# Modulation stretches at the highest priority, the half loaded last first, and four PSUM banks for the products instead of five

## The chip, the cores and the metric

The kernel runs on one core of a Trainium2 chip. The metric is the time of one execution on the device in microseconds (us). Five engines work side by side, each in its own fixed order: TensorE (PE in the profile; PEld is its weight load), VectorE (DVE), ScalarE (ACT), GpSimd (POOL), and SyncE (SP), which here only issues DMAs. They meet through semaphores.

## The reference

One layer of a decoder is computed for two groups that share all weights: a prompt of 256 tokens and a sample group of 8 sequences with one new token each, together 264 columns. The model width is 2048, all data are float32. In short:

```
mod = silu(c) @ w_ada + b_ada                  # c: 1 + 8 rows; six parts of 2048: sh1 sc1 gt1 sh2 sc2 gt2
h = rmsnorm(x) * (1 + sc1) + sh1
q, k, v, u, ga, gb = split(h @ w_in)           # 9216 columns
o = dilated window attention, 12 heads in three groups (prompt: over itself; sample: over a cache)
p = multi-scale causal pooling of u, a linear map per group, a scale
x = x + gt1 * ((sigmoid(ga) * (o @ w_up_attn) + sigmoid(gb) * (p @ w_up_pool)) @ w_out)
h2 = rmsnorm(x) * (1 + sc2) + sh2
x = x + gt2 * (square(relu(h2 @ w_mlp_up)) @ w_mlp_down)
y = rmsnorm(x)                                 # and the updated caches of keys, values and pool inputs
```

## The kernel before, in words

**The products.** Each large matrix product holds the weights as the stationary operand, in tiles of 128 x 128, and streams the 264 columns. Weights and activations are each split into a high part of reduced precision and the rest: ACT casts the loaded weights to `whi` (L228), DVE subtracts to get `wlo` (L229), in pieces of 128 x 1024. A product is then three matmuls, L239 (high x high), L240 (high x rest) and L241 (rest x high), into one PSUM bank of the pool `mm`. In the text "a product" is one of these matmuls; there are 10,752 of them. Loads of 1 MB go through a pool of five buffers named `raw`, all issued by SP in the order of the program; a load is issued when the buffer it takes is free, either because DVE has split the weights that lay there or because PE has read them.

**The modulation.** `mod` is a product with 9 rows only, so there the loaded weights are the moving operand and `cT`, the 32-column block with silu(c), is the stationary one. Four such matmuls with 32 columns each run side by side in the array (`tile_position`), one for each quarter of the output, into the bank `pa`: L294 in `ada_pair`, which makes the first two parts in chunks of 1, 1, 2, 2, 2, 4 and 4 blocks of 128, just ahead of the chunk of `w_in` rows that needs them, and L345 in `ada_part`, which makes the other four parts in the background of the later stages, two loads at a time. `burst` gathers the matmuls of two loads and issues those of the second load first, the others behind them: a stretch of 32, 16 or 8 matmuls. The profile counts two records for one of them, so a stretch of 8 is x16 there. When a part is complete, ACT copies the sums to `adasb` (L251), PE turns them by transposes (L258, L315) into a bank of `mm`, and DVE adds the bias into `mods` (L263, L266).

**The stages.** The head (up to 22 us) loads x, transposes it (L436), computes the row norms and the first modulation chunk. Then come the first 5120 columns of `w_in` in seven chunks of rows, each accumulated into `qkv` by DVE, ACT or POOL as a bank fills (L516 to L526; a bank is filled by 3 products in the first two chunks, by 6 or 12 in the later ones); then the gates with pooling and the attention of the prompt woven between (L594 to L674), the attention of the sample (from L796 on), whose cache is loaded by DMAs that POOL issues (L700), then the products with `w_up_pool`, `w_up_attn` and `w_out`, and the MLP. After `w_out`, DVE and ACT update x, square it and add the squares into `sqa` (L914); PE sums the rows (L425, L426) for the second norm, and the first MLP products need `h2hi` and `h2lo`, which hold besides the activations ten columns with a part of `mods`.

**What sets the order.** The code is written in program order, and a scheduler of the framework puts each engine's instructions into the order that is executed. It follows a model of the engines and DMAs: of the instructions that are ready in the model, the one with the highest priority goes next, and without further notice that is the one written first. `tc.issue_after(i)` lets what is issued in the block come behind `i` on its engine. `tc.high_priority()`, which the change uses, puts what is issued in the block ahead of everything else that is ready. PSUM has eight banks: `psm` gives MB of them to products (name `mm`), `psa` one to the modulation (`pa`), and `psx` the remaining 7 - MB to all else, transposes and attention above all (`px`). The lines of the diff are L49, L268 to L274 and L288.

Of the kernel before, what the change touches and what calls it, by code (L numbers as in the profile page):

```python
# [45 lines left out]
UPR = 1  # L46
WO = (2, 3)
TW = (1, 3)
MB = 5  # L49
PI, PM = 4, 3  # L50
WARM = 6

# [70 lines left out]
def step_kernel(ctx, tc, x_prompt, x_sample, vectors, c_sample, kv0, kv1, kv2, state_pool, w_ada, w_in, w_up_attn,  # L123
# [12 lines left out]
    wsp = ctx.enter_context(tc.tile_pool(name="wsp", bufs=3))  # L136
    psm = ctx.enter_context(tc.tile_pool(name="psm", bufs=MB, space=bass.MemoryType.PSUM))
    psa = ctx.enter_context(tc.tile_pool(name="psa", bufs=1, space=bass.MemoryType.PSUM))
    psx = ctx.enter_context(tc.tile_pool(name="psx", bufs=7 - MB, space=bass.MemoryType.PSUM))

    def mm_tile(n=N):
        return psm.tile([128, 512], F32, name="mm")[:, :n]
# [102 lines left out]
    def flush():  # L245
        while pending:
            pending.pop()()

    def ada_block(src, cols):
        sb = adap.tile([128, 512], F32, name="adasb")  # L250
        nc.scalar.copy(sb[:, :cols], src[:, :cols])  # L251
        return sb

    def turn(sb, n):

        p = mm_tile(n * 128).rearrange("p (j c) -> p j c", j=n)
        for j in range(n):
            nc.tensor.transpose(p[:, j], sb[:, j * 128:(j + 1) * 128], ident)  # L258
        return p

    def set_mods(part, d0, m, p):
        n = m.shape[1]
        nc.vector.tensor_add(m, p, bT[:, part * 16 + d0:part * 16 + d0 + n, None].to_broadcast([128, n, 9]))  # L263
        if part in (1, 4):
            gv = (g_mix if part == 1 else g_mlp)[:, d0:d0 + n, None].to_broadcast([128, n, 9])
            nc.vector.tensor_mul(m, m, gv)  # L266

    def burst(raws, emit):  # L268

        last = emit(*raws[-1])  # L270
        for r in raws[:-1]:
            with tc.issue_after(last.ins):
                last = emit(*r)
        raws.clear()  # L274

    def ada_pair(d0, n, per=2):

        w = n * 128
        k = 1024 // w
        pa = psa.tile([128, 512], F32, name="pa")  # L280
        cols = 128 if n == 1 else w // 2
        each = KT // 2 if n == 1 else KT
        done = [0] * 4
        raws = []

        def emit(s, raw):
            for j in range(0, k, 2 if n == 1 else 1):
                for g in range(4):  # L288
                    if n == 1:
                        kt, src = s + j + g % 2, raw[:, g // 2, j + g % 2]  # L290
                    else:
                        kt, src = s + j, raw[:, g // 2, j, g % 2 * cols:(g % 2 + 1) * cols]
                    done[g] += 1
                    i = nc.tensor.matmul(pa[32 * g:32 * g + 32, :cols], cT[:, kt], src, start=done[g] == 1,  # L294
                                         stop=done[g] == each, tile_position=(0, 32 * g))
            return i

        for s in range(0, KT, k):
            raw = rawp.tile([128, 2048], F32, name="raw").rearrange("p (a k c) -> p a k c", a=2, k=k)
            for a in range(2):  # L300
                c0 = a * D + d0 * 128
                nc.sync.dma_start(raw[:, a], w_ada[s * 128:(s + k) * 128, c0:c0 + w].rearrange("(k p) c -> p k c", p=128))
            flush()
            raws.append((s, raw))
            if len(raws) == per:
                burst(raws, emit)
            if s + k < KT:
                yield
        sb = ada_block(pa, cols)

        def finish():
            nb = cols // 128
            if n == 1:
                p = mm_tile()[:, :18].rearrange("p (a b) -> p a b", b=18)
                nc.tensor.matmul(p[:, 0], sb[:, :128], sel2, start=True, stop=True)  # L315
                for part in range(2):
                    set_mods(part, d0, mods[:, part * 16 + d0:part * 16 + d0 + 1], p[:, :, part * 9:part * 9 + 9])
                return
            p = turn(sb, nb)
            for g in range(4):  # L320
                part, half = divmod(g, 2)
                dd = d0 + half * nb
                set_mods(part, dd, mods[:, part * 16 + dd:part * 16 + dd + nb], p[:, :, 32 * g:32 * g + 9])

        pending.append(finish)
        yield
# [9 lines left out]
    def ada_part(part):  # L336
# [12 lines left out]
        for kt in range(KT):  # L349
            v = load(w_ada[kt * 128:(kt + 1) * 128, part * D:(part + 1) * D], 1, D)  # L350
            flush()
            raws.append((kt, v))
            if len(raws) == 2:
                burst(raws, emit)
            if kt + 1 < KT:
                yield
# [320 lines left out]
    for kv in range(-1, 2):  # L677
        p = px([96, 128])
        nc.tensor.transpose(p, small[:, 1 + kv].rearrange("p h b -> p (h b)"), ident)
        r = ap.tile([96, 128], F32, name="rows", bufs=3)  # L680
# [364 lines left out]
    last = adap.tile([128, 512], F32, name="adasb")  # L1045
# [54 lines left out]
```

## Time and profile before

| | us |
|---|---|
| median of 3 runs | 1510.38 |
| lowest, highest | 1508.73, 1510.42 |
| the profiled execution | 1508.2 |
| its span, first to last instruction | 1506.4 |
| PE busy | 1484.2 |
| DVE busy | 875.4 |
| ACT busy | 668.3 |

Busy time counts from the start to the end of an instruction; matmuls overlap, so the time that a matmul costs is read from the start of one to the start of the next, not from its duration. Of an engine that waits, the profile tells how long it was idle and which instruction or DMA ended that. [...]

### The profile page before, as it was taken

What the parts mean: (1) busy time and instruction counts of PE and PEld (TensorE: products, weight loads), DVE (VectorE), ACT (ScalarE), POOL (GpSimd) and SP (SyncE); (2) the same over time, 40 slices, a digit from 0 to 9 for tenths busy, and PEclk for the clock granted to TensorE, in tenths of its full rate; (3) what the DMA queues carried; (4) which work ended last, traced back from release to release, by engine and by line L of the source; (5) the groups of instructions that cost most, each with busy time, mean ns of one, the idle gap of its engine ahead of it and who ended that gap; (6) DMA issues with size and microseconds to landing.
All of it is one profiled execution on the core that took longest, in us unless ns stands there. A gap on an engine that the chain in (4) does not pass through costs nothing.

```text
span 1506.4 us, 29357 instructions
## 1 busy us (share of the span) xinstructions
PE 1484.2 (99%) x12454; PEld 1398.6 (93%) x12454; DVE 875.4 (58%) x1404; ACT 668.3 (44%) x992; POOL 114.6 (8%) x175
## 2 busy tenths in 40 slices
PE   7999999999999999999999999999999999999997
PEld 6899999877899889899999999999999999999997
DVE  6876666544465437765855445545555555555765
ACT  5544433344444544454644444344343444434355
POOL 0334100010101001300000000000010000100000
PEclk9999999999999999999999999999999999999998
DMA  9979998888897778877666666677576685766541
GB/s 302 323 267 315 330 310 286 313 289 265 281 312 263 255 259 301 289 265 263 217 226 224 224 224 224 227 237 249 169 265 224 210 293 174 274 228 245 205 141 58
DMA packets 162931, 377.62 MB, mean 251 GB/s; under 512 B 7233, under 2 KB 33361, under 8 KB 153192
## 3 DMA queue, kind: packets, MB, share of 16 engines
q1 hardware_dynamic: 153152, 340.02, 65.8%
q0 software_dynamic: 4064, 33.03, 6.0%
q10 hardware_dynamic: 5584, 2.69, 0.6%
q8 instruction: 98, 1.61, 0.4%
q14 instruction: 33, 0.27, 0.0%
HBM read 370.74 MB, written 26.15 MB: 263 GB/s over the span
## 4 chain that ended last, share of the span: by engine, by line
PE 97%; ACT 1%; DMA 1%; DVE 0%; issue 0%; SPq 0%; ACTq 0%
PE mm L239 29%; PE mm L240 29%; PE mm L241 29%; PE pa L345 4%; PE pa L294 2%; PE px L654 1%; PE px L672 1%; DMA raw<-in_w_ada_dram 1%; PE px L636 0%; ACT whi L228 0%; PE px L1012 0%; PE px L667 0%; PE px L436 0%; PE px L833 0%; PE mm L258 0%
## 5 line engine op out<-in xcount | busy, mean ns | idle before, releaser
L229 DVE TENSOR_TENSOR wlo<-raw,whi 128x1024 fp32r<-128x1024 f32 x448 | 555.4, 1241 | 468.3 <-ACT whi L228 463.4
L228 ACT CAST whi<-raw 128x1024 fp32r<-128x1024 f32 x448 | 469.5, 1049 | 630.1 <-PE mm L240 541.0
L239 PE MATMUL mm<-hhi,whi 128*128 128x264 f32 x1152 | 331.8, 289 | 3.1 <-ACT whi L228 2.2
L240 PE MATMUL mm<-hlo,whi 128*128 128x264 f32 x1152 | 328.8, 286 | 0.0
L241 PE MATMUL mm<-hhi,wlo 128*128 128x264 f32 x1152 | 326.3, 285 | 0.0
L239 PE MATMUL mm<-h2hi,whi 128*128 128x264 f32 (+1 forms) x1024 | 292.1, 285 | 0.0
L241 PE MATMUL mm<-ffhi,wlo 128*128 128x264 f32 x1024 | 291.9, 285 | 0.0
L240 PE MATMUL mm<-h2lo,whi 128*128 128x264 f32 (+1 forms) x1024 | 291.7, 285 | 0.0
L240 PE MATMUL mm<-fflo,whi 128*128 128x264 f32 x1024 | 291.6, 285 | 0.0
L239 PE MATMUL mm<-ffhi,whi 128*128 128x264 f32 x1024 | 291.4, 285 | 0.0
L241 PE MATMUL mm<-h2hi,wlo 128*128 128x264 f32 (+1 forms) x1024 | 291.3, 285 | 0.0
L239 PEld LDWEIGHTS mm<-hhi,whi 128*128 128x128 f32 x1152 | 217.2, 189 | 19.9 <-issue 12.7
L240 PEld LDWEIGHTS mm<-hlo,whi 128*128 128x128 f32 x1152 | 217.5, 189 | 1.2 <-DVE gate_a L526 0.8
L241 PEld LDWEIGHTS mm<-hhi,wlo 128*128 128x128 f32 x1152 | 216.4, 188 | 0.3 <-issue 0.2
L239 PEld LDWEIGHTS mm<-h2hi,whi 128*128 128x128 f32 x1024 | 193.2, 189 | 4.2 <-ACT whi L228 2.5
L239 PEld LDWEIGHTS mm<-ffhi,whi 128*128 128x128 f32 x1024 | 193.5, 189 | 1.7 <-ACT xa L998 0.8
L240 PEld LDWEIGHTS mm<-fflo,whi 128*128 128x128 f32 x1024 | 193.5, 189 | 0.0
L241 PEld LDWEIGHTS mm<-h2hi,wlo 128*128 128x128 f32 x1024 | 192.6, 188 | 0.8 <-DVE wlo L229 0.8
L240 PEld LDWEIGHTS mm<-h2lo,whi 128*128 128x128 f32 x1024 | 192.8, 188 | 0.0
L241 PEld LDWEIGHTS mm<-ffhi,wlo 128*128 128x128 f32 x1024 | 192.4, 188 | 0.0
L239 PE MATMUL mm<-mhi,whi 128*128 128x264 f32 x256 | 73.5, 287 | 0.0
L240 PE MATMUL mm<-mlo,whi 128*128 128x264 f32 x256 | 72.8, 284 | 0.0
(279 smaller groups left out, 1379.9 us busy)
## 6 DMA issues: line engine op xcount, KB each, us to landing
raw<-in_w_in_dram SPq DMA_DIRECT2D x71, 1024.0 KB, 7.1
raw<-in_w_ada_dram SPq DMA_DIRECT2D x64, 1024.0 KB, 5.3
raw<-in_w_mlp_up_dram SPq DMA_DIRECT2D x64, 1024.0 KB, 5.5
raw<-in_w_mlp_down_dram SPq DMA_DIRECT2D x64, 1024.0 KB, 5.1
raw<-in_w_ada_dram SPq DMA_DIRECT2D x64, 512.0 KB, 6.9
raw<-in_w_out_dram SPq DMA_DIRECT2D x16, 1024.0 KB, 7.4
cv<-in_cache_kv_w_dram POOLq DMA_DIRECT2D x5, 1024.0 KB, 10.0
raw<-in_w_up_pool_dram SPq DMA_DIRECT2D x4, 1024.0 KB, 7.2
```

The lines of the kernel that those rows point to most:

```text
L228: nc.scalar.copy(hi, v)
L229: splits.append(nc.vector.tensor_sub(lo, v, hi.bitcast(F32)))
L239: nc.tensor.matmul(ps, wh, x[0][:, kt, :n], start=start, stop=False)
L240: nc.tensor.matmul(ps, wh, x[1][:, kt, :n], start=False, stop=False)
L241: nc.tensor.matmul(ps, wl, x[0][:, kt, :n], start=False, stop=stop)
L294: i = nc.tensor.matmul(pa[32 * g:32 * g + 32, :cols], cT[:, kt], src, start=done[g] == 1, stop=done[g] == each, tile_position=(0, 32 * g))
L345: i = nc.tensor.matmul(pa[32 * g:32 * g + 32], cT[:, kt], v[:, 0, g * 512:(g + 1) * 512], start=done[0] == 1, stop=done[0] == KT, tile_pos ...
L654: nc.tensor.matmul(p, qkv[:, hd, qt * 128:(qt + 1) * 128], qkv[:, 12 + hd, :nk * 128], start=True, stop=True)
L672: nc.tensor.matmul(po, qkv[:, 24 + 4 * g + slot, kb * 128:(kb + 1) * 128], pt[:, g, kb], start=kb == 0 and g == 0, stop=kb == nk - 1 and g ...
```

## The change

MB goes from 5 to 4, so the products have four banks and `px` three. The matmuls of `burst` are issued with the highest priority. In `ada_pair`, for stretches over two loads, the quarters 2 and 3, which read the half of a load that is issued second, come ahead of the quarters 0 and 1.

```diff
-MB = 5
+MB = 4
...
     def burst(raws, emit):
 
-        last = emit(*raws[-1])
-        for r in raws[:-1]:
-            with tc.issue_after(last.ins):
-                last = emit(*r)
+        with tc.high_priority():
+            last = emit(*raws[-1])
+            for r in raws[:-1]:
+                with tc.issue_after(last.ins):
+                    last = emit(*r)
         raws.clear()
...
-                for g in range(4):
+                for g in (2, 3, 0, 1) if per > 1 else range(4):
```

The order of the DMAs on SP and of everything on POOL stays. PE's order changes in many places, and with it that of ACT and DVE. Three places follow. Lines after L270 have a number higher by one in the changed kernel.

PE in the attention of the prompt, before: `pa` is the modulation, L636 the transposes of keys and values, L654 the scores.

```order
L636 MATMUL px<-cst_76,qkv 128x128 x4
L654 MATMUL px<-qkv 128x128
L345 MATMUL pa<-raw,cT 32x512
L654 MATMUL px<-qkv 128x128
L345 MATMUL pa<-raw,cT 32x512 x4
L654 MATMUL px<-qkv 128x128
L345 MATMUL pa<-raw,cT 32x512 x3
```

The same place now:

```order
L346 MATMUL pa<-raw,cT 32x512 x8
L625 MATMUL px<-z,wpool 128x264 x4
L637 MATMUL px<-cst_76,qkv 128x128 x18
L241 MATMUL mm<-hhi,wlo 128x264
L239 MATMUL mm<-hhi,whi 128x264
```

The eight matmuls of a stretch stand together and earlier, ahead of the pooling's map (L625) and of the transposes.

PE ahead of the sample's attention scores, before: the first transposes of that attention (L796) stand among products, the next stretch of the modulation 144 products behind them.

```order
L239 MATMUL mm<-hhi,whi 128x264
L240 MATMUL mm<-hlo,whi 128x264
L241 MATMUL mm<-hhi,wlo 128x264
L796 MATMUL px<-cst_76,s_4837 32x128
L797 MATMUL px<-cst_4835,s1p 32x64
L798 MATMUL px<-cst_4835,s2p 32x16
```

Now the same stretch stands here, 13 products ahead of those transposes:

```order
L239 MATMUL mm<-hhi,whi 128x264
L240 MATMUL mm<-hlo,whi 128x264
L346 MATMUL pa<-raw,cT 32x512 x8
L241 MATMUL mm<-hhi,wlo 128x264
L239 MATMUL mm<-hhi,whi 128x264
```

It moved forward by 157 products. So did six of the seven stretches of the MLP; the others moved forward by 13 to 144, but for the one of the second chunk, which is whole now at about its place.

PE at the start of the MLP, before: the row sums stand 27 products behind the last product with `mhi` or `mlo`, the operands of `w_out`.

```order
L241 MATMUL mm<-h2hi,wlo 128x274
L425 MATMUL px<-cst_76,sqa 128x1 x2
L426 MATMUL px<-sqa,cst_76 128x8
L425 MATMUL px<-cst_76,sqt 128x1 x2
L426 MATMUL px<-sqt,cst_76 128x8
```

Now:

```order
L241 MATMUL mm<-mhi,wlo 128x264
L239 MATMUL mm<-h2hi,whi 128x274 x3
L426 MATMUL px<-cst_76,sqa 128x1 x2
L427 MATMUL px<-sqa,cst_76 128x8
L239 MATMUL mm<-h2hi,whi 128x274
L426 MATMUL px<-cst_76,sqt 128x1 x2
L427 MATMUL px<-sqt,cst_76 128x8
L240 MATMUL mm<-h2lo,whi 128x274
```

DVE at that place, now, where L904 and L906 empty a bank of `w_out`, L915 adds into `sqa`, L403 reads the row sums, and L234 from `mods` writes the ten columns of `h2lo`:

```order
L229 TENSOR_TENSOR wlo<-raw,whi 128x1024
L915 TENSOR_TENSOR sqa<-sqa,sqt 128x264
L930 TENSOR_TENSOR xa<-xT,mods 128x8
L904 TENSOR_TENSOR rt<-mm,mods 128x8
L906 SCALAR_TENSOR_TENSOR xT<-mm,mods,xT 128x256
L234 TENSOR_TENSOR h2lo<-xa,h2hi 128x264
L905 TENSOR_TENSOR xT<-xT,rt 128x8
L403 TENSOR_SCALAR rsv<-px 128x10
L930 TENSOR_TENSOR xa<-xT,mods 128x8
L234 TENSOR_TENSOR h2lo<-mods,h2hi 128x16x9
```

The row sums moved up to the third product of the MLP, and the columns from `mods`, which stood ahead of the last four outputs of `w_out` on DVE, come behind them. The transposes that turn this part of `mods` moved from 96 products ahead of the end of `w_out` to 24.

## Rows read from the trace of the kernel before

**Rows 1.** The page: busy time of the engines with their share of the span, and the granted clock of PE in 40 slices of the span, in tenths.

```profile
PE 1484.2 (99%) x12454; PEld 1398.6 (93%) x12454; DVE 875.4 (58%) x1404; ACT 668.3 (44%) x992; POOL 114.6 (8%) x175
...
PEclk9999999999999999999999999999999999999998
```

**Rows 2.** The waits of PE: engine, tile and line, what ended the wait; us in total, how many, the longest.

```profile
PE px L208 <- DVE sl L201: 5.6, 1, 5.6
PE px L1060 <- DVE adasb L1058: 3.0, 1, 3.0
PE mm L239 <- ACT whi L228: 2.2, 2, 1.8
PE mm L258 <- ACT adasb L251: 2.0, 4, 0.7
PE pa L294 <- DMA raw<-in_w_ada_dram: 0.9, 1, 0.9
```

**Rows 3.** PE in order of time around an undivided stretch in the MLP: start, duration, line, operands, count.

```profile
983.93 0.28 PE L240 MATMUL mm<-h2lo,whi 128*128 128x264 f32 x1
984.05 0.28 PE L241 MATMUL mm<-h2hi,wlo 128*128 128x264 f32 x1
984.27 1.92 PE L345 MATMUL pa<-raw,cT 128*32 128x512 f32 x16
986.12 0.39 PE L239 MATMUL mm<-h2hi,whi 128*128 128x264 f32 x1
```

**Rows 4.** The same view of a divided stretch in the attention.

```profile
320.36 1.05 PE L345 MATMUL pa<-raw,cT 128*32 128x512 f32 x2
321.34 0.49 PE L654 MATMUL px<-qkv 128*128 128x128 f32 x2
321.75 1.07 PE L345 MATMUL pa<-raw,cT 128*32 128x512 f32 x8
322.75 0.49 PE L654 MATMUL px<-qkv 128*128 128x128 f32 x2
```

**Rows 5.** The same view of a piece of one in the first chunk.

```profile
31.80 0.41 PE L294 MATMUL pa<-raw,cT 128*32 128x128 f32 x2
32.14 0.39 PE L241 MATMUL mm<-hhi,wlo 128*128 128x264 f32 x1
```

**Rows 6.** The head: the issue of the last modulation load (SPq is the queue of SP) and, from the list of DMA issues of that moment, its size and the us from issue to landing; then the matmuls that read it, in PE's order of time.

```profile
9.68 1.60 SPq L302 DMA_DIRECT2D raw<-in_w_ada_dram  x1
...
raw<-in_w_ada_dram SPq DMA_DIRECT2D x1, 512.0 KB, 7.5
...
18.48 1.08 PE L294 MATMUL pa<-raw,cT 128*32 128x128 f32 x32
```

**Rows 7.** The same three views at the sample's attention: issue and landing of the second load of the stretch that begins at 514.59, the first transposes of the attention, and that stretch.

```profile
488.17 0.34 SPq L219 DMA_DIRECT2D raw<-in_w_ada_dram  x1
...
raw<-in_w_ada_dram SPq DMA_DIRECT2D x1, 1024.0 KB, 8.6
...
494.56 0.41 PE L796 MATMUL px<-cst,s 128*32 128x128 f32 x2
...
514.59 1.92 PE L345 MATMUL pa<-raw,cT 128*32 128x512 f32 x16
```

**Rows 8.** The same views in the attention of the prompt: a stretch, and issue and landing of the second of the two loads that it releases.

```profile
345.25 1.92 PE L345 MATMUL pa<-raw,cT 128*32 128x512 f32 x16
...
347.23 0.33 SPq L219 DMA_DIRECT2D raw<-in_w_ada_dram  x1
...
raw<-in_w_ada_dram SPq DMA_DIRECT2D x1, 1024.0 KB, 7.7
```

**Rows 9.** The same views in the MLP: issue and landing of the second load of the stretch at 798.60, that stretch, and issue and landing of the second load of the next one, which begins at 835.7.

```profile
774.66 0.34 SPq L219 DMA_DIRECT2D raw<-in_w_ada_dram  x1
...
raw<-in_w_ada_dram SPq DMA_DIRECT2D x1, 1024.0 KB, 5.7
...
798.60 0.64 PE L345 MATMUL pa<-raw,cT 128*32 128x512 f32 x4
...
811.79 0.34 SPq L219 DMA_DIRECT2D raw<-in_w_ada_dram  x1
...
raw<-in_w_ada_dram SPq DMA_DIRECT2D x1, 1024.0 KB, 4.7
```

**Rows 10.** PE and DVE in order of time at the start of the MLP: its first product, and DVE's last addition into `sqa`.

```profile
722.15 0.29 PE L239 MATMUL mm<-h2hi,whi 128*128 128x274 f32 x1
...
724.91 0.42 DVE L914 TENSOR_TENSOR sqa<-sqa,sqt 128x264 f32<-128x264 f32 x1
```

**Rows 11.** Groups of DVE's instructions: busy us and mean ns of one, and the idle time ahead of them with what ended it. The split of the weights, and the emptying of a bank in the first chunk.

```profile
L229 DVE TENSOR_TENSOR wlo<-raw,whi 128x1024 fp32r<-128x1024 f32 x448 | 555.4, 1241 | 468.3 <-ACT whi L228 463.4
...
L516 DVE TENSOR_SCALAR qkv<-mm 128x264 f32<-128x264 f32 x18 | 7.6, 430 | 3.2 <-PE mm L241 3.1
```

**Rows 12.** Busy time of the engines in stretches at the end of the head: the stretch and its length in us, then PE, PEld, DVE, ACT and POOL with their instruction counts, the granted clock of PE as a share, the share of the DMA engines and GB/s.

```profile
20.00:22.00 2.00, 0.60 (x6) 0.36 (x4) 1.41 (x8) 1.14 (x2) 0.00 (x0) 1.00 1.26 302
22.00:23.00 1.00, 0.55 (x2) 0.55 (x3) 0.96 (x3) 1.00 (x2) 0.00 (x0) 0.65 1.08 349
23.00:24.00 1.00, 1.00 (x7) 1.00 (x6) 1.00 (x2) 0.35 (x1) 0.00 (x0) 0.50 1.04 419
...
25.00:26.00 1.00, 1.00 (x8) 1.00 (x6) 0.69 (x3) 0.67 (x2) 0.00 (x0) 0.65 1.14 317
```

## The prediction

> **What bounds the kernel now.** I read the page's busy shares first: TensorE (PE) is busy 1484.2 of 1506.4 us, the next engine 58% [rows 1]. The reader is to see that no stage waits for DVE, ACT or the DMAs for long. Then the waits of PE: the five largest are 13.7 us together, 8.6 of it at the two ends, and one alone, 0.9 us, is for a load [rows 2]. So only three things can move the time: what PE spends between the products (the lines L239 to L241, 0.12 us from start to start [rows 3]), the waits it gets, and the head. The profiled execution took 1508.2 us and its span 1506.4, so 1.8 us lie outside; the median of the three runs shown is 1510.4, that is 2.2 above the profiled one. I work out the difference on the profiled one and add it to the median.
>
> What stands between products is mostly the modulation: 640 matmuls of 32 columns, four at a time side by side. An undivided stretch of eight takes from 984.27 to the next product at 986.12, 1.85 us [rows 3]. In the attention one of those eight alone takes 0.98 us (320.36 to 321.34) and four take 1.00 (321.75 to 322.75) [rows 4]: the price goes by begun fours, so each division costs nearly a microsecond.
>
> **The change part by part.** The high priority joins the pieces; by the order of the changed program all stretches but the first chunk's are whole.
> - Attention: three stretches stood as 1+4+3, two as 5+3 or 1+7. The first kind is three begun fours of 0.98 to 1.00, some 2.96 instead of 1.85 us, 1.11 more [rows 3, 4]; in the second kind the longer piece still holds two begun fours, and the other adds some 0.98. 3 x 1.11 + 2 x 0.98 = 5.3 us gone.
> - Two stretches elsewhere, around 238 and 755, had one matmul split off. The seven left are still two begun fours: 2 x 0.98 gone [rows 4], and a little of the return to the products, 2.1 us.
> - In the first chunks a piece of one runs from 31.80 to the product at 32.14, 0.34 [rows 5]; a piece of two, elsewhere, I put at 0.5 as an estimate from it. 0.8 us gone.
> - After a stretch, PE waited for ACT's copy of the sums before it turned them: 2.0 us in four waits [rows 2]. In the new order these transposes stand 35 to 135 products behind their stretch. 2.0 us gone (0 if the bank they need is what they wait for).
> - Head: the last modulation load is issued at 9.68 and lands 7.5 later, 17.2; its 16 matmuls start at 18.48 because the transposes of x, on two px banks, stand before them [rows 6]. With three banks the transposes pass earlier. At most 1.3 us (18.48 - 17.2), at least 0; I take 1.0, nearer the upper end, because nothing else stands before them.
>
> Sum gone: 5.3 + 2.1 + 0.8 + 2.0 + 1.0 = 11.2 us. Nothing hides it, for PE is the bound.
>
> What is late next: the stretches also move forward, to where the scheduler holds their loads for landed. PE is served in order, so where the load is later than that, all products behind the stretch wait. Before, the stretches stood well behind: 514.59 and 798.60 are both some 18 us after the landing of the second load [rows 7, 9].
> - Sample attention: the order now has a stretch 13 products ahead of L796. Those 13 start to start put it at 494.56 - 13 x 0.12 = 492.9 in the time of before [rows 7]. Its second load is issued at 488.17, released by the same split of DVE in both programs, and lands 8.6 later, 496.8, because the cache loads that POOL issued share the DMA engines; before, its stretch began at 514.59 [rows 7]. A wait of 3.9 us; 0 if POOL's loads come earlier, hardly more.
> - Attention: where a stretch's two loads are both released by the stretch ahead of it, the second is issued 2.0 us after that one starts and lands 7.7 later, 9.7 after it [rows 8]. In the new order the distances, counted in products and transposes, are about 8.9 to 10.6 us. Five such places: 0 to 1.6 us each; I take 0.3, 1.5 together.
> - MLP: the stretch at 798.6 moves 157 products forward (19.1 us), to 779.5; its load lands at 774.66 + 5.7 = 780.4, 0.9 us [rows 9]. The one before it, divided around 755, stands alike, 0.9. The next, at 835.7, goes to 816.6 against 811.79 + 4.7 = 816.5 [rows 9], and the following four stand the same way, at nothing. With 0.2 for these, 2.0 us; up to 3 if each is a little late.
> - Elsewhere (early chunks, gates, pooling and output projection) the distance from the releasing split to the stretch is 28 to 60 products, 3.4 to 7.3 us, against 4.7 for a lone load [rows 9]: one place of 28 at 1.3 us, the rest near 0. I take 1.7 (0 to 5).
> - Start of the MLP: the order now has the row sums (L425) three products behind the output projection, where it had 27. They read sqa, whose last addition ends at 725.3, while the first MLP product started at 722.15 [rows 10]: 725.3 less 722.5 is 2.8 us of wait. DVE's new order has one weight split (1.24 us) less before that addition but four mods additions more, and the low parts of mods, which the next products need, now follow it. I take 2.3 (0 to 3.7). The late mods come from the four banks: with no spare one their transposes wait until two of the projection's banks are empty.
> - Four banks: in the first two chunks a bank is filled by three products, 0.37 us. DVE's split takes 1.24 and its emptying of a bank 0.43 [rows 11], so a bank behind a split is empty 1.67 us later; three further banks give 1.1 us, four gave 1.46. Each of ten such meetings may cost 0.37 more, 3.7 at most, 0 at least. The order has shifted the splits between the emptyings, as before, and PE hardly waits there now; I take 0.4. From the third chunk on a bank takes 0.73 us or more, and three of them (2.2) cover 1.67.
>
> Sum added: 3.9 + 1.5 + 2.0 + 1.7 + 2.3 + 0.4 = 11.8 us. Net +0.6: 1508.8 for the profiled execution, 1511.0 us against the median.
>
> **The rivals.**
> - *The loads are there in time.* The scheduler's distances agree with the measured landing of a lone load to 0.1 us in the MLP, which speaks for it; against it, it did not see POOL's loads at 488. Then only the sample-attention wait and 1.5 us of all the other waits stay: -11.2 + 3.9 + 1.5 = -5.8, 1504.6 us.
> - *The clock falls after the waits* (the slower side). [...] 2 x 1.6 beside landings at the upper bounds (attention +1.0, elsewhere +1.5): 1511.0 + 5.7 = 1516.7 us. It decides if a wait in the middle counts as the idle time at 20 to 22 did. Against it: the page shows no other fall before the end [rows 1].
> [...]
> - *Banks.* PE runs dry behind the splits of the first two chunks at the upper bound, +3.3 over my value: 1514.3 us. For it speaks that DVE is busiest there; against it, that PE's waits for the splits are 2.2 us in all, most of it ahead of the first product [rows 2].
>
> **How the numbers follow.** The forecast, 1511.0 us, has a chance of 0.40; loads in time 0.32; the clock 0.18; banks 0.10. About 0.2% (3 us) is what a measurement of this kernel can tell from no change, so the bounds are 1507.4 and 1513.4: the forecast's own range is that of "same", the first rival is faster, the other two slower. Faster 0.32, same 0.40, slower 0.28. The range goes from 1503 (all loads in time but one, the head at its upper bound) to 1518 (the clock and some more).
>
> **What would show it.** Right: 16 records of pa at each place and no piece of two; a wait of pa for a load ahead of L796 of 3 to 4 us; PE idle 2 to 3 us before the row sums; the first product near 21.4. Wrong: no wait of pa for a load over 1 us (then it is faster), or half-clock stretches after 30 us, or PE waits for qkv or gate_a of the first chunks over 2 us.

## The result, and the profile after

| us | before | after |
|---|---|---|
| median (4 runs each) | 1509.56 | 1528.61 |
| lowest, highest | 1508.33, 1510.42 | 1526.94, 1531.37 |
| the profiled execution, its span | 1508.2, 1506.4 | 1529.8, 1528.1 |

The change makes the kernel slower: ratio 1.0129, 95% interval 1.0117 to 1.0140. That is 19.1 us by the medians and 21.6 by the two profiled executions, of which the one of before lies 1.4 under its median and the one of after 1.2 over. The page of after, PE's busy time and granted clock [rows 1]:

```profile
PE 1485.9 (97%) x12454; PEld 1406.5 (92%) x12454; DVE 874.3 (57%) x1404; ACT 669.6 (44%) x992; POOL 119.5 (8%) x175
...
PEclk9999999999999999999999999999999999999998
```

The page shows almost nothing: as many instructions of PE, PE busy for 1485.9 us against 1484.2 [rows 1], and a clock row with no digit changed, for a short fall vanishes in a slice of 38 us. The time is in the waits. PE's waits in after, columns as in [rows 2]:

```profile
PE pa L346 <- DMA raw<-in_w_ada_dram: 9.7, 7, 3.6
PE px L208 <- DMA cst<-in_consts_dram: 5.9, 1, 5.9
PE px L1061 <- DVE adasb L1059: 3.0, 1, 3.0
PE mm L239 <- ACT whi L228: 2.6, 2, 2.4
PE mm L239 <- ACT phi L233: 2.3, 1, 2.3
PE mm L240 <- DVE hlo L234: 2.1, 2, 1.5
PE px L668 <- ACT sc L663: 1.3, 1, 1.3
PE pa L295 <- DMA raw<-in_w_ada_dram: 1.3, 3, 0.7
PE px L426 <- ACT sqt L913: 0.8, 2, 0.5
...
PE px L426 <- DVE sqa L915: 0.7, 1, 0.7
```

All listed waits make 34.3 us, against 15.6 in before. The stretches' waits for their loads, 0.9 us once [rows 2], are now 11.0 us in ten. The second largest new group is products and row sums that wait for ACT and DVE (phi, hlo, sqa, sqt): no load is late there.

The largest single place answers to [rows 7]: issue and landing of the stretch's second load, the stretch, and the sample's transposes.

```profile
492.53 0.34 SPq L219 DMA_DIRECT2D raw<-in_w_ada_dram  x1
...
raw<-in_w_ada_dram SPq DMA_DIRECT2D x1, 1024.0 KB, 8.4
...
500.99 2.69 PE L346 MATMUL pa<-raw,cT 128*32 128x512 f32 x16 [3.56 <-DMA raw<-in_w_ada_dram]
503.61 0.59 PE L241 MATMUL mm<-hhi,wlo 128*128 128x264 f32 x1
504.00 0.42 PE L239 MATMUL mm<-hhi,whi 128*128 128x264 f32 x1
...
506.19 0.41 PE L797 MATMUL px<-cst,s 128*32 128x128 f32 x2
```

The load lands at 500.9 and the stretch starts with it, 3.56 us late. But the stretch then takes 2.69 us where it took 1.92, and a product 0.42 where it took 0.28 [rows 3]: the granted clock of PE is 0.50 of full speed there (503 to 505 us). The windows of after show where it falls once the head is over (columns as in [rows 12]):

```profile
68.00:70.00 2.00, 2.00 (x14) 2.00 (x12) 1.49 (x3) 0.39 (x1) 0.37 (x1) 0.63 1.05 351
70.00:72.00 2.00, 2.00 (x38) 1.65 (x41) 1.05 (x2) 0.00 (x0) 0.38 (x1) 0.52 0.40 134
501.00:503.00 2.00, 2.00 (x16) 0.40 (x16) 0.00 (x0) 0.00 (x0) 0.00 (x0) 0.75 0.91 351
503.00:505.00 2.00, 2.00 (x10) 1.39 (x7) 0.00 (x0) 0.00 (x0) 0.00 (x0) 0.50 1.00 272
505.00:507.00 2.00, 2.00 (x22) 1.85 (x21) 0.03 (x1) 0.83 (x1) 0.00 (x0) 0.89 0.95 323
...
577.00:579.00 2.00, 1.65 (x7) 1.65 (x8) 1.31 (x2) 1.98 (x2) 0.00 (x0) 0.53 0.23 90
579.00:581.00 2.00, 2.00 (x13) 2.00 (x12) 0.68 (x2) 0.46 (x2) 0.00 (x0) 0.62 0.03 12
...
740.00:744.00 4.00, 3.49 (x18) 3.28 (x19) 3.32 (x13) 1.86 (x5) 0.00 (x0) 0.62 0.80 259
744.00:748.00 4.00, 4.00 (x22) 4.00 (x20) 0.40 (x3) 0.00 (x0) 0.19 (x1) 0.53 0.03 7
```

Busy time times the missing share of the clock gives 1.7, 1.7, 1.5 and 3.2 us, 8.2 in all (at 501: 2.00 x 0.25 + 2.00 x 0.50 + 2.00 x 0.11). In before the clock stays at 1.00 from 26 to 1496 us. So 18.7 us more waits and 8.2 of clock make 26.9, and the span grew by 21.7: some 5 us net were gained elsewhere.

Each half-clock stretch follows a wait of PE, but only one of them a wait for a load (at 67.39 us it had waited 1.53 us for `hlo`, which DVE writes). At 576 us, in PE's order of time, after:

```profile
573.51 0.28 PE L241 MATMUL mm<-hhi,wlo 128*128 128x264 f32 x1
576.06 0.75 PE L239 MATMUL mm<-phi,whi 128*128 128x264 f32 x4 [2.27 <-ACT phi L233]
577.35 0.59 PE L240 MATMUL mm<-plo,whi 128*128 128x264 f32 x1 [0.54 <-DVE plo L234]
```

and the same place before:

```profile
560.13 0.28 PE L241 MATMUL mm<-hhi,wlo 128*128 128x264 f32 x1
560.34 1.92 PE L345 MATMUL pa<-raw,cT 128*32 128x512 f32 x16
562.19 0.74 PE L239 MATMUL mm<-phi,whi 128*128 128x264 f32 x4
563.38 0.39 PE L240 MATMUL mm<-plo,whi 128*128 128x264 f32 x1 [0.44 <-DVE plo L234]
```

A stretch used to stand here, and ACT made `phi` beside it. It has moved 158 products forward, from product 3456 to 3298 (the text ahead of the prediction puts such moves at 13 to 157; by the order of PE's records in the two traces they go up to 168). The next one stands at 3409, 47 products ahead of `phi`, so the wait that was covered is open. The row sums wait for another reason besides: they stand at product 4611, where they stood at 4635 (answering to [rows 10]; PE, after):

```profile
739.91 0.60 PE L426 MATMUL px<-cst,sqa 128*128 128x1 f32 x4 [0.66 <-DVE sqa L915]
...
741.49 1.02 PE L426 MATMUL px<-cst,sqt 128*128 128x1 f32 x4 [0.51 <-ACT sqt L913]
```

To place the loss I compare the start of the nth product in both traces. After is behind by 7.0 us at product 1440 (end of `ada_pair`), 4.4 at 2304 (end of the attention) and at 2976, 11.3 at 3264 (sample scores done), 15.4 at 3552 (behind phi), 15.6 at 4560, 23.1 at 4752 (MLP begun), 21.6 at the end.

### The profile page after: what moved, and what is told of

Same layout as the page of the kernel before. It is cut to its first block, busy times and chain, and to the rows that moved or that the text cites. A ratio compares the mean times of both kernels' runs of the same rounds, so it can differ in the third digit from the quotient of the medians.

```text
span 1528.1 us, 29391 instructions
## 1 busy us (share of the span) xinstructions
PE 1485.9 (97%) x12454; PEld 1406.5 (92%) x12454; DVE 874.3 (57%) x1404; ACT 669.6 (44%) x992; POOL 119.5 (8%) x175
## 3 DMA queue, kind: packets, MB, share of 16 engines
q10 hardware_dynamic: 5584, 2.69, 0.6%
## 4 chain that ended last, share of the span: by engine, by line
PE 84%; DMA 8%; DVE 4%; ACT 2%; issue 1%; POOL 0%; ACTq 0%; SPq 0%; DVEq 0%; POOLq 0%
PE mm L240 25%; PE mm L241 25%; PE mm L239 25%; DMA raw<-in_w_ada_dram 7%; PE pa L346 4%; DVE wlo L229 2%; PE pa L295 2%; ACT whi L228 1%; PE px L673 1%; PE px L655 0%; DMA qkv<-in_x_prompt_dram 0%; DMA qd<-rows 0%; PE px L437 0%; DMA out_dram<-sc 0%; POOL gate_b L887 0%
## 5 line engine op out<-in xcount | busy, mean ns | idle before, releaser
L228 ACT CAST whi<-raw 128x1024 fp32r<-128x1024 f32 x448 | 469.7, 1049 | 657.6 <-PE mm L240 642.3
L346 PE MATMUL pa<-raw,cT 128*32 128x512 f32 x512 | 63.1, 604 | 10.4 <-DMA raw<-in_w_ada_dram 9.7
```

What stands on the lines that cost most here:

```text
L228: nc.scalar.copy(hi, v)
L346: i = nc.tensor.matmul(pa[32 * g:32 * g + 32], cT[:, kt], v[:, 0, g * 512:(g + 1) * 512], start=done[0] == 1, stop=done[0] == KT, tile_pos ...
```

## The experiments

Two theories stood at the start. One: the early places cost, by waits for loads, by waits that they uncover, and by the clock. The other: the four banks cost.

**Banks and priority apart (e1, e2).** e1 is the change with five banks, e2 the kernel before with four.

```diff
-MB = 4        # e1, in the changed kernel
+MB = 5
-MB = 5        # e2, in the kernel before
+MB = 4
```

> The changed kernel with five product banks again; priority and order of the halves stay. Theory (early stretches make PE wait for their loads, and the clock falls after the long waits): the waits stay, only the late mods ahead of the MLP go, worth about 5.5 us by the two traces: 1520 to 1526 us. Rival (the four banks are what costs): back to the kernel before or better, 1500 to 1510 us.

> The kernel before with four product banks and three others, nothing else. Theory: within 4 us of the kernel before, 1507 to 1514. Rival (four banks cost most of it): 1520 or more.

Measured: e1 1520.38 us, ratio 1.0072 (1.0057 to 1.0087); e2 1510.82, 1.0010 (1.0001 to 1.0019). Four banks alone cost 1.5 us (0.2 to 2.9). Most of the loss is the priority's; the 8 us between e1 and after need both. In e1 the row sums do not wait and show no half clock (with five banks the late modulations turn 72 products earlier, at 4512 and not 4584): from product 4560 to 4752 it falls back by 2.2 us, after by 7.5. That is 5.3 of the 8.

**Whole stretches held at their old places (e3, e4).** Priority and order of halves stay, but a stretch may not pass the last product written before it. e3 has five banks, e4 four.

```diff
-        nc.tensor.matmul(ps, wl, x[0][:, kt, :n], start=False, stop=stop)
+        done_mm[:] = [nc.tensor.matmul(ps, wl, x[0][:, kt, :n], start=False, stop=stop)]
...
-        with tc.high_priority():
+        with ExitStack() as held:
+            held.enter_context(tc.high_priority())
+            if done_mm:
+                held.enter_context(tc.issue_after(done_mm[0].ins))
             last = emit(*raws[-1])
```

> Five banks, high priority, but each stretch is also held behind the last product written before it, so it is whole and stands where the kernel before has it, 8 to 19 us behind its load. Theory: no wait for a load, no clock fall in the middle, and the 8 to 10 us of the joined pieces and of the turning appear: 1499 to 1503 us. Rival (joining gains nothing, PE pays the same elsewhere): 1507 to 1511. If the load waits do not matter it is no faster than e1.

> As e3 with four banks: the changed kernel with nothing but the places of its stretches put back. Theory: 1500 to 1508 us, within 5 us of e3. Rival (four banks): 10 us or more above e3.

Measured: e3 1507.56 us, 0.9985 (0.9974 to 0.9996); e4 1504.82, 0.9969 (0.9960 to 0.9978), 24 us under after and faster than before. So the early places cost, not the priority as such. The same seven stretches of the attention as groups of PE, before (307.1 to 408 us) and e4 (309.5 to 405):

```profile
L345 PE MATMUL pa<-raw,cT 128*32 128x512 f32 x112 | 19.3, 602 | 0.0
```

```profile
L351 PE MATMUL pa<-raw,cT 128*32 128x512 f32 x112 | 13.5, 598 | 0.0
```

Five of the seven were divided in before, and PE is busy with them 5.8 us less when they are whole. From the start of each piece to the start of what follows it, the five took 14.6 us; whole, at 1.85 each, they take 9.3, so 5.3 us less. e3 gained less than expected because there the attention waited: 2.6 us at 327 for `qkv`, with a half-clock stretch behind it, and 1.1 at 387. That the pieces had filled such waits is not shown. Nor is it shown that the third bank for the attention removes them: e4 meets 0.8 us at most there, but e8 and e10, whose edits touch nothing in the attention, meet 1.6 and 1.8.

**Which half of the priority (e5, e6).** Priority in `ada_pair` alone, or in `ada_part` alone:

```diff
-    def burst(raws, emit):
+    def burst(raws, emit, first=False):
...
-        with tc.high_priority():
+        with ExitStack() as held:
+            if first:
+                held.enter_context(tc.high_priority())
...
+                burst(raws, emit, True)      # in ada_pair (e5) or in ada_part (e6)
```

> The change, with the priority given in ada_pair alone; the stretches of ada_part have their old priority, and stand at the places that they have with four banks alone. In the trace of after, the lag behind before is 7.0 us at product 1440, where the last stretch of ada_pair is done, and that of four banks alone is 1.8 there: the difference, 5.2, is this part's price. Theory (early places cost where they stand, and the parts add up): four banks alone plus 5, 1516 (1513 to 1519). Rival (early places of ada_pair set off the later losses, since buffers and loads come earlier from there on): most of the 18 us, over 1522. Second rival (the early half was chance of one execution): 1510 to 1512.

> The change, with the priority given in ada_part alone; from product 1501 on every stretch and turning has the place that it has in after. Theory (the parts add up): after less 5, 1523.5 (1520 to 1527), with the waits of 3 to 4 us ahead of product 3011 and 2 us ahead of the products on phi, and half-clock stretches behind both and at the row sums, as in after. Rival (the losses hang on the early places of ada_pair): below 1515.

Measured: e5 1513.40 us, 1.0022 (1.0013 to 1.0031); e6 1525.77, 1.0102 (1.0087 to 1.0118). Against e2 (1510.8) that is 2.6 and 15.0, together 17.6; after stands 17.8 above e2. The parts add up. e5's waits for loads, and those of e6:

```profile
PE pa L297 <- DMA raw<-in_w_ada_dram: 6.1, 7, 1.3
```

```profile
PE pa L348 <- DMA raw<-in_w_ada_dram: 9.2, 12, 4.2
...
PE mm L239 <- ACT phi L233: 2.3, 1, 2.3
```

**One stretch let go from e4 (e7, e8, e10).** The edit is the same with another number: burst 30 now stands ahead of the sample scores (e7), 33 leaves the products on phi (e8), 42 leaves the row sums (e10).

```diff
+            bursts.append(1)
-            if done_mm:
+            if done_mm and len(bursts) != 30:      # 33, 42
                 held.enter_context(tc.issue_after(done_mm[0].ins))
```

> The held version with four banks (1504.8), with one stretch let go: the first one behind the sample scores, which then stands ahead of product 3011, as in after, and not at 3168. Its second load lands at 494.0 us by the trace of the held version, and product 3011 ends near 490.7. Theory (a wait for the load, and behind it a stretch at half clock): 3.3 + 1.7 = 5.0, so 1509.8 (1508.5 to 1511). Rival (the wait alone costs): 1508.1, without a half-clock stretch near 500 us. Second rival (what is lost there is made up where the stretch no longer stands, and the loss in after has other causes): 1504 to 1506.

> The held version with four banks (1504.8), with one other stretch let go: the one that stood at product 3456, ahead of the first products on phi, now stands at 3380. Its load has landed by then or lands within 1 us. Theory (a stretch moved ahead uncovers the wait that it stood before: phi 2.3 and plo 0.5, less the 0.5 that waits there already, and 1.7 for the clock behind it): 3 to 4 us, so 1508.3 (1507 to 1510), with no wait for a load above 1 us. Rival (only waits for loads cost): 1504 to 1506.

> The held version with four banks (1504.8), with one stretch let go: the one at product 4560, ahead of the row sums, now at 4475; the turning of the late modulations stands at 4584, as in after. Its load lands in time or within 1 us. Theory (the stretch covered the wait of the row sums, and without it they wait 1 to 1.5 us as in after, and the clock falls behind them, 1.7 to 3.4): 3 to 5 us, 1508.8 (1507 to 1510.5). Rival (the row sums lose only behind all the earlier places together, by loads that share the queue): 1504 to 1506.

Measured: e7 1510.55 us, 1.0007 (0.9998 to 1.0017), 5.7 over e4; e8 1508.61, 0.9991 (0.9982 to 1.0001), 3.8 over; e10 1508.42, 0.9991 (0.9980 to 1.0002), 3.6 over. PE in e7:

```profile
487.84 0.28 PE L242 MATMUL mm<-hlo,whi 128*128 128x264 f32 x1
492.38 3.64 PE L354 MATMUL pa<-raw,cT 128*32 128x512 f32 x16 [4.26 <-DMA raw<-in_w_ada_dram]
...
497.00 0.42 PE L241 MATMUL mm<-hhi,whi 128*128 128x264 f32 x1
```

The wait is 4.26 us, the clock takes the rest: the granted clock is 0.50 from 492 to 496 us and 0.56 on the mean of 496 to 498, the stretch takes 3.64 us where it took 1.92, and the products are slow (0.42 us for 0.28) until 497.7. By the traces this place costs 6.9 us. PE in e8 and, below, a window of it:

```profile
557.20 0.28 PE L243 MATMUL mm<-hhi,wlo 128*128 128x264 f32 x1
559.74 1.05 PE L241 MATMUL mm<-phi,whi 128*128 128x264 f32 x4 [2.27 <-ACT phi L233]
...
560.00:562.00 2.00, 1.75 (x8) 1.44 (x8) 1.31 (x2) 1.98 (x3) 0.00 (x0) 0.50 0.78 324
```

No load is late here (1.0 us of waits for loads, none of them at this place), and yet one moved stretch costs 3.7 us: a cover taken away is as dear as a load waited for. e10's time met the expectation, its trace did not: the row sums wait (0.63 and 0.51), but the clock stays at 1.00 there, and the place costs 1.3 us. The rest of the 3.6 has no place in the edit; the two intervals allow a difference from 0.3 to 6 us. The pair also differs in more than the cover: with the stretch held the row sums stand at product 4624 (e4, e15), with it let go at 4611 (e10, after). e10's profiled execution lost 2.5 us in the attention, which the edit does not touch: PE waits there for DVE, and the clock falls behind it.

```profile
721.90 0.61 PE L434 MATMUL px<-cst,sqa 128*128 128x1 f32 x4 [0.63 <-DVE sqa L923]
...
722.00:726.00 4.00, 3.49 (x27) 3.28 (x28) 3.59 (x14) 1.86 (x5) 0.00 (x0) 1.00 0.76 246
...
318.87 0.49 PE L663 MATMUL px<-qkv 128*128 128x128 f32 x2 [1.79 <-DVE sc L665]
...
320.00:322.00 2.00, 2.00 (x10) 2.00 (x11) 0.84 (x2) 1.43 (x2) 0.00 (x0) 0.50 0.67 191
```

**The wait of e7 filled with work (e9, e13).** 32, then 18 matmuls of zeros into the same sum, behind product 3011 and ahead of the stretch:

```diff
+            if len(bursts) == 30:
+                held.enter_context(tc.issue_after(done_mm2[1003].ins))
+                for q in range(32):      # 18
+                    nc.tensor.matmul(pa[:32, :128], zero, ident, start=False, stop=False,
+                                     tile_position=(0, 0))
```

> e7 once more (the held version with one stretch ahead of product 3011), with 32 matmuls of zeros ahead of that stretch: they add nothing to its sum, need no load, and take 0.12 us each by the two of 128 columns at the sample scores of e7, 3.8 us of the 4.3 us that TensorE waits there. Theory (the wait costs its own length, and TensorE idle that long loses its clock besides: in e7 the stretch took 3.64 us against 1.94, and the products behind it ran at half clock until 497.7): the load lands no earlier, the wait shrinks to about 0.5 us, there is no half-clock stretch, and 2.4 us of e7's 1510.6 come back: 1508.2 (1507 to 1509.2). Rival (the clock falls for what comes in by the load, or the stretch itself is slower at this place): 1510.6, with the half-clock stretch.

> e9 with 18 matmuls of zeros in place of 32. In the trace of e9 each of the 32 stands as two records of 0.11 us: they took 7.1 us (488.4 to 495.5), not 3.8, so they covered the wait of 4.3 us and then held the stretch up; 18 take 4.0. There was no half-clock stretch in e9. Theory (the clock falls because TensorE stands idle): still none near 500 us, the stretch in 1.9 to 2.0 us, and the loss of that place (e7: 6.9 us by the traces) comes down to the wait of 4.3 plus what the zeros overhang: 1508 (1507 to 1509.5). Rival (the filling costs as much as the clock, whatever its length): 1510.5 to 1511.5.

Measured: e9 1511.12 us, 1.0010 (1.0002 to 1.0019); e13 1509.68, 0.9997 (0.9987 to 1.0007). PE in e13, and two windows of it:

```profile
491.68 4.01 PE L282 MATMUL pa<-cst,zero 128*32 128x128 f32 x35
...
495.63 1.88 PE L360 MATMUL pa<-raw,cT 128*32 128x512 f32 x13
497.44 0.39 PE L243 MATMUL mm<-hhi,wlo 128*128 128x264 f32 x1
...
493.00:495.00 2.00, 2.00 (x21) 2.00 (x20) 0.00 (x0) 0.00 (x0) 0.00 (x0) 1.00 0.82 270
495.00:497.00 2.00, 2.00 (x24) 1.21 (x21) 0.00 (x0) 0.00 (x0) 0.00 (x0) 1.00 0.95 355
```

With PE busy through the wait the clock does not fall at this place: it is 1.00 in e13, where e7 had 0.50, and in e9 the last 13 records of the stretch take 1.88 us as in e13. From product 2976 to 3024 e13 is 2.9 us faster than e7. So at this place the fall hangs on PE's idle time, not on the load. e9 missed its time because I had taken one record for one matmul: each stands as two of 0.11 us, so the zeros lasted 7.1 us and gave back what the clock returned. e13's median lies 0.9 under e7's, 0.2 above its range; its profiled execution lost 3 to 4 us before 70 us, at a wait of 2.78 us for ACT's `adasb` with a half-clock stretch behind it (mean granted clock of that execution 0.993). e9, with the same edit there, has neither (0.996). The trace of the place settles it, the time alone would not.

**The order of the halves (e11, e12).** e11 is e4 with `range(4)` again, e12 the kernel before with `(2, 3, 0, 1)`.

> The held version with four banks, without the change's order of the halves: range(4) again, so the half loaded last is read third and fourth. Theory (with every load 8 us and more ahead of its stretch the order within it decides nothing): 1504.8 (1503.8 to 1506). Rival (the order is part of what the held version gains): over 1506.5.

> The kernel before with the order of the halves alone. Theory: nothing, 1509.5 (1508.5 to 1510.5). Rival (the wait for the half that comes last is now met first in the few stretches of before whose loads land late, and a stretch that can't start loses more than one that stops in its middle): over 1510.5.

Measured: e11 1505.11 us, 0.9969 (0.9957 to 0.9981); e12 1509.89, 1.0000 (0.9990 to 1.0009). The order of the halves does nothing in these two kernels; in the changed kernel, where loads are waited for, it was not tried.

**The changed kernel with some stretches held (e14, e15).** The edit of e3, for 13 of 49 stretches (e14) or for one (e15):

```diff
+            if 30 <= len(bursts) <= 42:      # e15: the 42nd alone
                 held.enter_context(tc.issue_after(done_mm[0].ins))
```

> The change, with thirteen of its stretches held behind the product written before them: those from the sample scores to the row sums (products 3168 to 4560). All others stand where after has them: in ada_pair, in the attention and in the products of the MLP. Theory (the losses lie where the early places uncover waits, and add up): after (1528.6) less what its trace loses against before between products 2976 and 4752, 18.7 us (lag 4.4 to 23.1), plus 1.9, since the stretch at 4751 then still stands before its old place, plus what the held version loses there, 1.8: 1512.5 to 1514. Rival (what is saved there is lost again behind, because the loads of the MLP come later): over 1518.

> The change, with the stretch ahead of the row sums alone held (at 4560 in place of 4403). In after, lag 15.6 at product 4560 grows to 21.1 at 4660: 1.4 us of waits at the row sums and a stretch of 6.8 us at half clock. In e10 the same waits stood in the trace without the half clock, and cost 1.2. Theory (in after the clock falls there for these waits, because TensorE has stood idle shortly before as well): with the cover back no half clock near 740 us, 1528.6 less 5: 1523.5 (1522 to 1525.5). Rival (the half clock there has another cause, and only the 1.4 us come back): 1526.5 to 1528.

Measured: e14 1512.81 us, 1.0017 (1.0008 to 1.0026), as expected: 16 of the 19 us come back with 13 stretches, and nothing is lost again behind. e15: 1525.64, 1.0101 (1.0085 to 1.0117), 3.0 under after and 0.1 outside its range. PE at e15's row sums, and a window:

```profile
740.14 0.50 PE L434 MATMUL px<-cst,sqa 128*128 128x1 f32 x4
...
740.73 0.58 PE L434 MATMUL px<-cst,sqt 128*128 128x1 f32 x4
...
740.00:744.00 4.00, 4.00 (x35) 4.00 (x34) 2.27 (x8) 1.57 (x3) 0.00 (x0) 1.00 0.78 264
```

No wait, no half clock. Between products 4560 and 4660 it gains 4.1 us on after. As in e4, the row sums stand 13 products later than in after, so the run shows what this stretch's place is worth, but not how much of it is cover and how much the order.

## Why the prediction was wrong

1511.0 us was forecast, 1528.6 came, outside the range. By its own steps:

- **Waits for loads: right in sum, partly by luck.** 3.9 + 1.5 + 2.0 + 1.7 = 9.1 us were added; the traces show 11.0 less the 0.9 that was there, 10.1. The wait ahead of the sample scores was to be 3.9 and is 3.56 (4.26 in e7). The attention (0.3 for 1.5) and the MLP (1.1 for 2.0) wait less than put down; the rest, `ada_pair` and the gates above all, waits 6.1 us (0.9 of it there before), where "elsewhere" was to be 1.7.
- **Whole stretches: right.** The attention's 5.3 us came as 5.3. With the 2.1 and 0.8 elsewhere 8.2 us were counted; from start to next start, waits left out, all stretches together took 99.0 us in before and take 91.9 in after, 1.6 of it by the half clock, so some 8.6 were gained.
- **The turning wait (2.0 gone) and the head (1.0 gone).** The wait of L258 is gone from the list, but products wait for `hlo` (1.5 in a first chunk, 0.6 at 245 us; none listed before), so on balance nothing came of it. The first product starts at 22.42, before at 22.45: no gain.
- **Four banks, 0.4:** 1.5 us alone (0.2 to 2.9), too low but small. The remark that without a spare bank the late modulations' transposes wait until banks of the projection are empty was, by e1, the part that mattered: 5.3 of the 8 us between e1 and after lie there.
- **Start of the MLP, 2.3:** the waits are 1.45 us in all (0.28, 0.66, 0.51), within 0 to 3.7. The 3.2 us of half clock behind them were left out of the sum. e15 shows that this loss hangs on one stretch.
- **The step that failed is "What is late next", with the clock put at nothing.** It asked of each moved stretch whether its own load is late at the new place, and nowhere, but for the row sums, what waits once the stretch is gone from the old one. The products on `phi` were not looked at: 2.3 and 0.5 us of waits and 1.5 of clock, 3.7 in e8, stood in no term. And each wait was priced at its length alone; the half clock behind four of them, 8.2 us, is the largest term that the sum lacked.
- **The clock rival (0.18) was the right mechanism.** I set it aside because the page shows no other fall before the end; but before had no wait of PE over 0.7 us between 28 and 1490 us, so that row could not speak against it. Its 1.6 us for one place is the share of the clock that is missing from 22 to 26 us in [rows 12]; no row of before shows it for a wait in the middle. There most places took about as much (1.7, 1.7, 1.5); the row sums took 3.2, and e7 2.6. It counted two places; there were four in this execution, three of them in e6 too. So its own time, 1516.7 us, was too low by 12.

The runs show what such a wait does: behind e7's 4.26 us for a load the stretch took 3.64 us where it took 1.92 in before; e8 shows the fall behind 2.27 us for `phi`, which is no load (0.50 from 560 to 562 us); and with matmuls of zeros in e7's wait it does not come (e9, and e13 at 1.00).

With what was measured in place of what was put down, the sum is + 10.1 (loads) + 1.45 (row sums) + 2.4 (phi and plo, less the 0.4 of before) + 4.7 (the other waits by which the lists differ) + 8.2 (clock) = 26.9; the span grew by 21.7, so 5.2 net came back. The starts of all of PE's instructions tell what is in it: the stretches gave 8.6 and the `px` matmuls 2.2, both without the half clock; against that the products took 4.3 more, likewise without it, and waits that the lists leave out 1.1. The 4.3 come mostly from products right ahead of a wait, 45 in after and 9 in before: such a product counts as busy for 0.28 us, to its modelled end, where the next product would start after 0.12 (a stretch after 0.21). A wait thus costs more than the idle time that is listed for it.

The other rivals fall: the loads are not in time (seven waits up to 3.56 us), and the banks' 1514.3 was a cost in the first two chunks, where e2 (1.5 us behind at product 300) is no worse than e3 with five (1.6). (The 2.2 us of waits that were held against this rival are waits for ACT's cast, L228, not for DVE's split.) The sign that I had named for "wrong", half-clock stretches after 30 us, is the one that came.

Open: why the clock fell at the row sums of after and e6 and not at e10's, with the same waits; and why the wait of 1.53 us for `hlo` at 67 us was followed by a half-clock stretch in after, but not in e5, e14 and e15, where it was as long. Between 28 and 1490 us the traces of all runs go both ways for single waits of 1.5 to 2.2 us: 3 of 17 were followed by half clock (1.53 in after, 1.79 in e10, 1.92 in e11).

## What to carry to other kernels

Work that fills an engine's waits has two prices when it is moved: its own inputs at the new place, and what it covered at the old one; look at what stood right behind it. With the highest priority a load's reader was left no slack here (in after about half of the stretches start within 0.1 us of the landing, and none over 3.7 behind it; before it was mostly 8 us or more), so if only the joining is wanted, give priority but hold the place, as e4 does. Price a wait of TensorE in the middle of dense work at its length and, where it was 2.27 us or more in these traces, at 1.5 to 3 us of clock besides.

## What the hardware showed that I had not expected

A single idle time of 2.27 us (e8) was enough for the clock to fall, to 0.50 from 560 to 562 us, in the middle of a kernel that had been dense for 500 us, while e5's seven waits for loads, of up to 1.3 us, left it alone. All twelve waits of 2.27 us and more between 28 and 1490 us, in all traces together, were followed by half clock, whatever they were for (a load for 4.26 us in e7 and 3.56 in after, `phi` for 2.27 in e8 and after). In e9 and e13 a float32 matmul of 128 columns stands as two records of 0.11 us in the profile and costs both: 32 of them took 7.1 us, 18 took 4.0.
